# Begun feed-forward and gate blocks: another block's first half between a block's two halves, and planner durations and ranks set per sequence

## The chip, the cores and the metric

The kernel runs as one program on one core of a Trainium2 chip. The metric is the device time of one execution in microseconds (us), as the median of several runs.

The core has five engines that work side by side, each through its own queue in order: TensorE (PE, matmul), VectorE (DVE), ScalarE (ACT), GpSimd (POOL) and SyncE (SP, which here issues the DMA transfers). Semaphores tie them together. An instruction that waits holds up everything behind it on its engine.

## The reference, cut to what matters

The layer is computed for two sequences of 512 tokens of width 1024 that share all weights: a prompt (s = 0) and a sample (s = 1).

```
x = x + 0.5 * swiglu(rms_norm(x, ffn1_norm), w_gate, w_up, w_down)       # width 2816 inside
h = rms_norm(x, mix_norm);  proj = h @ w_in
aq, ak, av, mq, mk, mv, gate_pre, o_pre, g_att, g_mlstm = split(proj)
att = gqa_block_attention(rope(rms_norm(aq)), rope(rms_norm(ak)), av)    # 8 heads of 64, 2 of keys and values
mem = mlstm_bidirectional(mq, mk, mv, gate_pre, bias, o_pre, head_norm)  # 4 heads of 128, both directions
merged = sigmoid(g_att) * (att @ w_up_att) + sigmoid(g_mlstm) * (mem @ w_up_mlstm)
x = x + merged @ w_out
x = x + 0.5 * swiglu(rms_norm(x, ffn2_norm), w_gate, w_up, w_down)
y = rms_norm(x, final_norm)
```

## The kernel before

**Products.** Every fp32 operand is split in two parts (high, and what is left), and each product is three matmuls: high with high, high with low, low with high. The high part is made on ACT and the low part on DVE; for a weight of 128 x 1024 that is L817 and L820 in the mixing block, L2086 and L2089 in the blocks below, L247 and L248 in the feed-forwards. The gates and the feed-forwards multiply by a scheme of seven products instead of eight over the two sequences: the activations are held as blocks B11, B21, B22 and sums T1 to T4, the weights likewise, and results are put together afterwards.

**Three stages in time.** The first feed-forward fills the first 646 us of the trace, the second the last 603 us; their instruction order is written out by hand. Between them lies the planned stage: the gates g_att and g_mlstm of both sequences (about 646 to 772 us), the mixing block of the prompt (to 1034 us), that of the sample (to 1408 us), and the begun part of the second feed-forward (to 1453 us).

**The planner** (`Plan`, L707 to L768) sets the order in the planned stage when the program is built. Each piece of work is a task with an engine, a duration, what it depends on, and slots that it needs and frees: `mm=3`, `ps=2`, `pt=2`, `o=1` are PSUM banks, `w=2` and `wr=4` weight buffers, `kr=2` rows that hold results until a DMA has stored them. An engine takes, among the tasks that could start by its model clock first, the one of lowest rank. The rank is a base value, plus 0.001 for each task entered earlier, plus an entry of the table `RANK` (L693) under the key "part engine function". Durations come from `ACT_STEP` and `DVE_STEP` (L774, L775) by width and from a count n; a matmul of 512 columns counts 0.227; a transfer is taken to land `LANDING` = 1.9 after its bytes have moved. The planner's numbers set the order only. On the chip an engine runs in that order, whenever its semaphores allow.

**A begun block** (`begun_block`, L2108) is the part of a block of results that needs only B11 and B21, the sample's sums being unready. There are eight for the gates (`begin_gates`, L2231, part "gates7") and seven for the second feed-forward (`begin`, L2339, part "begin"). Each has two halves. The first half is 12 matmuls on B11 into a new `mm` bank (`seven`, L2093; the matmul is L2100); then ACT copies the bank to a `kr` row (`out`, L2128) and a DMA stores it. The second half is 12 matmuls on B21 that add to the same bank, so they may start only when that copy has read it; then a second ACT instruction at L2128 (Tanh for the gates, Silu for the feed-forward) frees the bank. All matmuls of `seven` have the base rank FILL = 5.

**The sums** (`sums_stage`, L2133, parts "gsums" and "sums") run on the other engines beside the begun blocks: scaling of rows (ACT L2140, DVE L2141), turns, that is transposes on PE (L1690), their copies with a gain (ACT L2170), stores of copied halves to xn1buf for later (DMA, L2178), differences (DVE L2190) that overwrite those halves, and the high and low parts of each sum (`put_in`: ACT L2182, DVE L2185).

**The rest of the gates** (`gates_rest`, L2249) multiplies the sums with sums of weights made on DVE (`left_sums`, four instructions). Its first product, p1, waits for its weights, the sums of T2, and the last begun block (`begun_g[-1]`).

**The mixing block** (`mix(s, ...)`, L878 to L1640) names the parts of its work by `do.part` ("kv", "k", "q", "gates", "keys", "rotate", "attend", "memory" and so on), one name for both sequences. Lines of it that are spoken of: queries are normalised and rotated on DVE (L1097 to L1111, low part L1131), turned on PE (L1137) and copied on ACT (L1140); scores (L1213) pass Exp on ACT (L1225), which needs a table load there. In "memory", the squares of a head are turned (`sums_`, L1523), summed (`reduced`, L1527), their root taken by 11 DVE instructions (`rooted`, L172 to L167), spread on PE (`cast`, L188) and applied (`ended`, L1536). The up-projections (L838) are merged on DVE (L1381), which frees their `mm` bank.

## Time and profile before

| | |
|---|---|
| time, median of 3 runs (lowest to highest) | 2056.19 us (2055.44 to 2056.62) |
| time of the profiled execution | 2058.12 us |
| its span | 2056.0 us |
| mean granted clock of TensorE | 0.998 |
| PE busy | 2030.5 us, 99%, 9370 matmuls |
| DVE, ACT, POOL busy | 1599.3, 966.2, 27.3 us |
| bytes moved by DMA | 389.04 MB, mean 189 GB/s |

The span runs from the first to the last instruction; the execution's own time is 2.12 us longer. Matmuls are pipelined, so a busy row of PE shows each as about 0.39 us although they start some 0.23 us apart; an idle time of PE shown in brackets is therefore less than what the matmul came late by. The better measure is from one start to the next, against the pace of matmuls that wait for nothing. In the listings in order of time a row reads: start, us, engine, line, operation, out<-in, count, and in brackets the idle time before and what ended it.

### The profile page before, as it was taken

What the parts mean: (1) busy time and instruction counts of PE and PEld (TensorE: products, weight loads), DVE (VectorE), ACT (ScalarE), POOL (GpSimd) and SP (SyncE); (2) the same over time, 40 slices, a digit from 0 to 9 for tenths busy, and PEclk for the clock granted to TensorE, in tenths of its full rate; (3) what the DMA queues carried; (4) which work ended last, traced back from release to release, by engine and by line L of the source; (5) the groups of instructions that cost most, each with busy time, mean ns of one, the idle gap of its engine ahead of it and who ended that gap; (6) DMA issues with size and microseconds to landing.
All of it is one profiled execution on the core that took longest, in us unless ns stands there. A gap on an engine that the chain in (4) does not pass through costs nothing.

```text
span 2056.0 us, 26145 instructions
## 1 busy us (share of the span) xinstructions
PE 2030.5 (99%) x9370; PEld 1679.7 (82%) x9370; DVE 1599.3 (78%) x2536; ACT 966.2 (47%) x1613; POOL 27.3 (1%) x53
## 2 busy tenths in 40 slices
PE   9999999999999999999999999999999999999997
PEld 7788888888888788887888888887788888888886
DVE  7897878786797764897887885875888787776687
ACT  7444434342227533586645674655443444443224
POOL 0000000001000000000000000000000000000001
PEclk9999999999999999999999999999999999999999
DMA  9456455699774544322332512464464644379753
GB/s 338 169 172 232 174 195 197 246 363 354 251 249 158 205 147 158 104 61 83 130 122 102 191 62 93 144 222 142 138 228 156 231 163 154 134 296 396 268 201 139
DMA packets 148978, 389.04 MB, mean 189 GB/s; under 512 B 14736, under 2 KB 14752, under 8 KB 147056
## 3 DMA queue, kind: packets, MB, share of 16 engines
q1 hardware_dynamic: 147856, 385.31, 52.9%
q0 software_dynamic: 560, 1.26, 0.3%
q8 instruction: 74, 1.21, 0.2%
q10 hardware_dynamic: 432, 0.79, 0.1%
q14 instruction: 56, 0.46, 0.1%
HBM read 269.31 MB, written 118.00 MB: 188 GB/s over the span
## 4 chain that ended last, share of the span: by engine, by line
PE 92%; ACT 3%; DVE 3%; DMA 1%; issue 1%; SPq 0%; ACTq 0%; DVEq 0%
PE pss L290 18%; PE pst L290 12%; PE mm L838 10%; PE mm L290 9%; PE mm L544 8%; PE mm L868 7%; PE pst L544 4%; PE pss L544 4%; PE pss L2100 3%; PE pso L544 3%; PE pst L2100 2%; PE pso L868 2%; PE mm L2100 2%; PE pss L1213 1%; PE pst L1237 1%; PE pss L1429 1%
## 5 line engine op out<-in xcount | busy, mean ns | idle before, releaser
L290 PE MATMUL pss<-xc,w 128*128 128x512 f32 x1632 | 389.1, 390 | 0.0
L290 PEld LDWEIGHTS pss<-xc,w 128*128 128x128 f32 x1632 | 306.5, 188 | 63.6 <-ACT w L247 0.2
L247 ACT ACTIVATE w<-wr 128x1024 fp32r<-128x1024 f32 (+1 forms) x122 | 127.3, 1045 | 227.2 <-PE pst L290 128.1
L248 DVE TENSOR_TENSOR w<-wr,w 128x1024 fp32r<-128x1024 f32 (+1 forms) x122 | 146.8, 1205 | 63.7 <-ACT w L247 63.2
L290 PE MATMUL mm<-xc,w 128*128 128x512 f32 x792 | 192.3, 393 | 2.9 <-DVE w L248 1.8
L544 PE MATMUL mm<-w,rt 128*128 128x512 f32 x792 | 185.3, 390 | 0.0
L290 PEld LDWEIGHTS mm<-xc,w 128*128 128x128 f32 x792 | 149.4, 189 | 35.5 <-DVE w L248 2.2
L544 PEld LDWEIGHTS mm<-w,rt 128*128 128x128 f32 x792 | 148.6, 188 | 30.7
L290 PE MATMUL pst<-xc,w 128*128 128x512 f32 x528 | 127.2, 390 | 0.7 <-DVE xc L1814 0.7
L290 PE MATMUL pst<-xc,f 128*128 128x512 f32 x528 | 127.1, 390 | 0.0
L820 DVE TENSOR_TENSOR w<-wr,w 128x1024 fp32r<-128x1024 f32 (+1 forms) x80 | 93.6, 1172 | 30.0 <-ACT w L817 29.7
L290 PEld LDWEIGHTS pst<-xc,w 128*128 128x128 f32 x528 | 99.1, 188 | 21.6 <-DVE xc L1814 1.2
L290 PEld LDWEIGHTS pst<-xc,f 128*128 128x128 f32 x528 | 99.4, 188 | 20.6
L604 ACT ACTIVATE w<-t 128x512 fp32r<-128x512 f32 x82 | 51.6, 632 | 121.7 <-PE pst L544 63.6
L604 ACT ACTIVATE w<-wr 128x512 fp32r<-128x512 f32 x72 | 44.6, 631 | 128.6 <-PE pso L544 67.6
L544 PE MATMUL pss<-w,rt 128*128 128x512 f32 x396 | 94.4, 390 | 0.8 <-ACT w L604 0.8
L544 PE MATMUL pst<-w,rt 128*128 128x512 f32 x396 | 94.0, 389 | 0.0
L817 ACT ACTIVATE w<-wr 128x1024 fp32r<-128x1024 f32 (+1 forms) x80 | 80.6, 1013 | 25.1 <-PE mm L838 6.7
L2100 PE MATMUL mm<-xc,w 128*128 128x512 f32 x360 | 86.0, 394 | 4.2 <-ACT f L2128 4.2
L544 PEld LDWEIGHTS pss<-w,rt 128*128 128x128 f32 x396 | 74.3, 188 | 16.5 <-ACT w L604 1.2
L544 PEld LDWEIGHTS pst<-w,rt 128*128 128x128 f32 x396 | 74.4, 188 | 15.4
L2100 PEld LDWEIGHTS mm<-xc,w 128*128 128x128 f32 x360 | 66.7, 188 | 20.7 <-ACT f L2128 7.2
(409 smaller groups left out, 3906.3 us busy)
## 6 DMA issues: line engine op xcount, KB each, us to landing
rt<-rbuf SPq DMA_DIRECT2D x154, 512.0 KB, 5.7
rbuf<-t SPq DMA_DIRECT2D x72, 512.0 KB, 3.3
wr<-in_ffn_w_gate_dram SPq DMA_DIRECT2D x60, 512.0 KB, 4.2
wr<-in_w_in_cols_dram SPq DMA_DIRECT2D x48, 512.0 KB, 4.0
wr<-in_ffn_w_up_dram SPq DMA_DIRECT2D x44, 512.0 KB, 3.5
rbuf<-f SPq DMA_DIRECT2D x30, 512.0 KB, 3.8
rbuf<-tab SPq DMA_DIRECT2D x30, 512.0 KB, 4.0
wr<-in_ffn_w_down_dram SPq DMA_DIRECT2D x48, 256.0 KB, 5.7
```

What stands on the lines that cost most here:

```text
L247: pin(nc.scalar.activation(t[:, 0], src, AF.Copy))
L248: pin(V_.tensor_tensor(t[:, 1], src, f(t[:, 0]), op=ALU.subtract))
L290: pin(nc.tensor.matmul(p, a[:, k, :], xt[:, b, k, :], start=(first and k == 0 and i == 0), stop=(k == HK_ - 1 and i == 2), skip_group_chec ...
L544: nc.tensor.matmul(p, r[:, b, d * P:(d + 1) * P], u[:, a, :], start=(first and q == 0 and k == 0), stop=(q == len(us) - 1 and k == 2), ski ...
L604: nc.scalar.activation(hi, src, AF.Copy)
L817: own(nc.scalar.activation(c["hi"], c["raw"], AF.Copy))
L820: own(V_.tensor_tensor(c["lo"], c["raw"], f(c["hi"]), op=ALU.subtract))
L838: own(nc.tensor.matmul(b["p"], w_[:, k, cols], x_, start=(k == 0 and i == 0), stop=(k == n - 1 and i == 2)))
L868: own(nc.tensor.matmul(b[q][:, :N], x_[:, q * P:(q + 1) * P], w_[:, kl, :], start=(k == 0 and i == 0), stop=(k == KD - 1 and i == 2)))
L1213: own(nc.tensor.matmul(p, G["qT"][:, h, b * P:(b + 1) * P], G["kv"][:, h // 4 * 2 + j, :], start=(j == 0), stop=(j == 1)))
L1237: own(nc.tensor.transpose(p[:, b * P:(b + 1) * P], G["e", h, b // 2][:, b % 2, kb * P:(kb + 1) * P], ident))
L2100: own(nc.tensor.matmul(bank[name], left()[a][:, k, :], xcl[m][:, y, k, :], start=bool(first) and k == 0 and i == 0, stop=(k == HK_ - 1 and ...
```

## The change

It adds no instruction and removes none: both programs have 9370 matmuls, 7 loads of ACT tables and the same DMAs. It changes the planner's input in four ways.

1. `seven` takes `later`, added to the rank of its matmuls. `begun_block` passes 0.04 for its second half (`BEHIND`), which is as much as 40 tasks entered later.
2. p1 of `gates_rest` no longer waits for the last begun block.
3. Parts of the mixing block carry the sequence's number ("kv0", "kv1"), and the table `RANK` is replaced: 39 entries for both sequences become 49, nearly all for one sequence.
4. Some durations: `ACT_STEP` for 256, 384, 512 and 544 columns, and n of six chains of small DVE instructions.

```
-    RANK = {"gates7 ACT out": -6.5, "gates7 ACT p_high": -23.5, "gsums ACT copy": 0.19, "grest ACT a_high": -1.5,
...
+    RANK = {"gsums ACT copy": 2.5, "q0 SP w_fetch": -6.4, "q0 ACT w_high": -8.5, "gates0 PE turn_e": 45,
...
-    ACT_STEP = {8: 0.2, 32: 0.2, 128: 0.3, 256: 0.37, 384: 0.5, 512: 0.5, 544: 0.57, 1024: 0.97}
+    ACT_STEP = {8: 0.2, 32: 0.2, 128: 0.3, 256: 0.33, 384: 0.45, 512: 0.51, 544: 0.7, 1024: 0.97}
...
-        do.part = "kv"
+        do.part = f"kv{s}"
...
-        t = dve(8, k_root, [t], 1, n=24)
+        t = dve(8, k_root, [t], 1, n=20)
...
-        root_q = dve(32, hold("rq", lambda: rstd_cols(G["ssq"], 32, DA, own)), reds, 0, n=12)
+        root_q = dve(32, hold("rq", lambda: rstd_cols(G["ssq"], 32, DA, own)), reds, 0, n=18)
...
-        scaled = dve(32, scales, [u], 1, (), ["pt"], n=14)
+        scaled = dve(32, scales, [u], 1, (), ["pt"], n=20)
...
-            inv = dve(8, inverse, stt + [en_t], 0, n=4)
+            inv = dve(8, inverse, stt + [en_t], 0, n=5)
...
-            u = dve(8, rooted, [u], 0, n=24)
+            u = dve(8, rooted, [u], 0, n=20)
...
-    def seven(left, xcl, m, bank, deps, first, need=(), free=(), name="p", stop=None):
+    def seven(left, xcl, m, bank, deps, first, need=(), free=(), name="p", later=0.0):
...
-                       FILL, need if k == 0 and i == 0 else (), free if end else ())
+                       FILL + later, need if k == 0 and i == 0 else (), free if end else ())
         return t
+
+    BEHIND = 0.04
...
-                      () if a else ["mm"], ["w"] if a else ())
+                      () if a else ["mm"], ["w"] if a else (), later=a * BEHIND)
...
-        u = dve(512, left_sums, [*fetched, g_t], 2, ["lone"], n=4)
+        u = dve(512, left_sums, [*fetched, g_t], 2, ["lone"], n=5)
...
-        p1 = seven(lambda: part(wb["t"], 0), xg, T2_, bank, [wb_t, *sums_g[T2_], begun_g[-1]], PS, ["ps"], (), "Y")
+        p1 = seven(lambda: part(wb["t"], 0), xg, T2_, bank, [wb_t, *sums_g[T2_]], PS, ["ps"], (), "Y")
```

The new lines shift the numbers: L2100 becomes L2104, L2128 becomes L2134, L2140 becomes L2146, L2170 becomes L2176, L2182 becomes L2188, L1690 becomes L1694, L838 becomes L842, L1523 becomes L1527.

**First place: PE, the last begun blocks of the gates.** Before, with blocks mm_389 and mm_393; xc_313 is B11 (first half), xc_314 is B21 (second half):

```order
L2100 MATMUL mm_388_5062<-xc_313_4673,w_383_4976 128x512 x6
L2100 MATMUL mm_389_5099<-xc_313_4673,w_385_5016 128x512 x5
L2100 MATMUL mm_388_5062<-xc_314_4674,w_383_4976 128x512 x12
L2100 MATMUL mm_389_5099<-xc_313_4673,w_385_5016 128x512 x7
L2100 MATMUL mm_393_5140<-xc_313_4673,w_387_5057 128x512 x5
L2100 MATMUL mm_389_5099<-xc_314_4674,w_385_5016 128x512 x12
L2100 MATMUL mm_393_5140<-xc_313_4673,w_387_5057 128x512 x7
L2100 MATMUL mm_393_5140<-xc_314_4674,w_387_5057 128x512 x12
```

After, the last rows of the same blocks, there named mm_389 and mm_390:

```order
L2104 MATMUL mm_389_5096<-xc_313_4673,w_386_5034 128x512 x9
L2104 MATMUL mm_387_5058<-xc_314_4674,w_384_4996 128x512 x9
L2104 MATMUL mm_390_5131<-xc_313_4673,w_388_5078 128x512
L2104 MATMUL mm_387_5058<-xc_314_4674,w_384_4996 128x512
...
L2104 MATMUL mm_390_5131<-xc_313_4673,w_388_5078 128x512 x9
L2104 MATMUL mm_389_5096<-xc_314_4674,w_386_5034 128x512 x12
L2104 MATMUL mm_390_5131<-xc_314_4674,w_388_5078 128x512 x12
```

Before, 0 to 7 matmuls of the next block's first half stand between the end of a block's first half and the start of its second (5 for mm_388 and mm_389, none for mm_393). After, 24 stand there (12 of the second half of the block before, taken in turn with 12 of the first half of the block behind), and 12 for the last block.

**Second place: ACT, in the begun part of the second feed-forward.** L2140 is the scaling of rows, L2170 the copies of the turns, and the table load is that of Silu. Before:

```order
L2128 ACTIVATE f2_1413_11448<-mm_1435_11641 128x512
L2140 ACTIVATE rows_1408_11430<-rows_1408_11430,rs_1443_11685 128x2x512 x2
L2128 ACT_TABLE_LOAD
L2128 ACTIVATE f2_1413_11448<-mm_1435_11641 128x512
L2128 ACTIVATE f2_1413_11448<-mm_1437_11669 128x512
L2086 ACTIVATE w_1452_11739<-wr_1432_11597 128x1024
L2170 ACTIVATE t2_1416_11451<-pss_1450_11727,gain_3_94 128x512
L2170 ACTIVATE t2_1417_11452<-pst_1451_11734,gain_3_94 128x512
```

After:

```order
L2134 ACTIVATE f2_1413_11466<-mm_1435_11641 128x512
L2134 ACTIVATE f2_1413_11466<-mm_1437_11669 128x512
L2146 ACTIVATE rows_1405_11387<-rows_1405_11387,rs_1443_11685 128x2x512 x2
L2176 ACTIVATE t2_1416_11469<-pss_1450_11728,gain_3_94 128x512
L2176 ACTIVATE t2_1417_11470<-pst_1451_11733,gain_3_94 128x512
L2176 ACTIVATE t2_1416_11469<-pss_1452_11739,gain_3_94 128x512
L2176 ACTIVATE t2_1417_11470<-pst_1453_11745,gain_3_94 128x512
L2176 ACTIVATE t2_1418_11471<-pss_1454_11750,gain_3_94 128x512
L2188 ACTIVATE xc_1445_11716<-t2_1417_11470 128x1024
L2176 ACTIVATE t2_1418_11471<-pss_1456_11763,gain_3_94 128x512
L2134 ACT_TABLE_LOAD
L2134 ACTIVATE f2_1413_11466<-mm_1435_11641 128x512
```

The table load, the Silu and a weight split (L2086) stood ahead of the first copy of a turn; now the copies stand ahead of them.

**Third place: PE, the end of the sample's mixing block.** `att` and `mem` are what the up-projections read, pst_1351 holds the turned squares of the last head, pst_1362 its cast. Before:

```order
L1523 MATMUL pst_1351_11058<-ident_85,t2_1349_11050 128x128 x4
L838 MATMUL mm_1345_11028<-att_1049_9365,w_1329_10954 128x512 x2
L838 MATMUL mm_1353_11068<-mem_1191_10000,w_1348_11043 128x512 x9
L838 MATMUL mm_1360_11097<-mem_1191_10000,w_1348_11043 128x512 x9
L838 MATMUL mm_1361_11108<-att_1049_9365,w_1329_10954 128x512
L188 MATMUL pst_1362_11110<-ident_85,rs_1359_11089 128x128 x4
L838 MATMUL mm_1361_11108<-att_1049_9365,w_1329_10954 128x512 x11
L838 MATMUL mm_1364_11133<-mem_1191_10000,w_1350_11055 128x512 x3
L838 MATMUL mm_1353_11068<-mem_1191_10000,w_1348_11043 128x512 x3
```

After:

```order
L1527 MATMUL pst_1351_11053<-ident_85,t2_1349_11044 128x128 x4
L842 MATMUL mm_1348_11041<-att_1038_9329,w_1329_10952 128x512 x7
L842 MATMUL mm_1354_11070<-att_1038_9329,w_1329_10952 128x512 x12
L842 MATMUL mm_1360_11100<-mem_1201_10059,w_1347_11038 128x512 x4
L188 MATMUL pst_1362_11108<-ident_85,rs_1359_11088 128x128 x4
L842 MATMUL mm_1360_11100<-mem_1201_10059,w_1347_11038 128x512 x5
L842 MATMUL mm_1364_11123<-mem_1201_10059,w_1347_11038 128x512 x9
L842 MATMUL mm_1365_11136<-mem_1201_10059,w_1350_11049 128x512 x5
L842 MATMUL mm_1360_11100<-mem_1201_10059,w_1347_11038 128x512 x3
```

Before, the last block on `att` (mm_1361) ended right ahead of mm_1364, which needs one of the three `mm` banks while mm_1353 and mm_1360 still hold two. After, both last blocks on `att` (mm_1348 and mm_1354) are through before the blocks on `mem` begin.

More of the change, by code (lines that the diff above doesn't have):

```diff
@@ L978, in mix @@
         swap(k_set, (), ["x"])
-        do.part = "q"
+        do.part = f"q{s}"
         qraw, reds, sqs = [], [], []
@@ L1012, in mix @@
         box_t = swap([q_t], ["A"], ["bx", "bx"], box)
-        do.part = "gates"
+        do.part = f"gates{s}"
         Fs, Is, fa, Lt, et = [small(32, t) for t in ("Fs", "Is", "fa", "Lt", "et")]
@@ L1170, in out_gate @@
         def out_gate(h):
-            do.part = "out_gate"
+            do.part = f"out_gate{s}"
             def done(bk, t):
@@ L1202, in mix @@
             out_gate(h)
-        do.part = "attend"
+        do.part = f"attend{s}"
         exps, low, last_a = {}, {}, []
@@ L1386, in mix @@
             mem_qk(h, v_in)
-        do.part = "memory"
+        do.part = f"memory{s}"
         mem_in, mt_last, mem_banks, exps_all = [], [], [], []
@@ L1548, in mix @@
         box_free = swap(mem_in + exps_all, ["bx", "bx"], ["A", "A"])
-        do.part = "before"
+        do.part = f"before{s}"
         fresh_in = before([att_free])
@@ L1560, in mem_gate @@
         def mem_gate(i):
-            do.part = "mem_gate"
+            do.part = f"mem_gate{s}"
             def g_fetch():
@@ L1590, in mix @@
         if s:
-            do.part = "last"
+            do.part = f"last{s}"
             swap(w3, ["qk", "qk"], ["w", "w"])
```

40 lines of the change are left out of this document (19 added, 21 removed), and 6 rows, old and new, of the table RANK.

## The prediction

> **What bounds the kernel.** I read the page first, then the waits of PE by line, then the stages, then PE, ACT and DVE in order of time around each wait.
>
> ```profile
> PE 2030.5 (99%) x9370; PEld 1679.7 (82%) x9370; DVE 1599.3 (78%) x2536; ACT 966.2 (47%) x1613; POOL 27.3 (1%) x53
> PE 92%; ACT 3%; DVE 3%; DMA 1%; issue 1%; SPq 0%; ACTq 0%; DVEq 0%
> ```
>
> PE is busy 99% of the span and carries 92% of the chain that ended last. The change leaves PE its 9370 matmuls, so only PE's waiting can move. Where it waits (engine, line, what for: us in total, times, longest us):
>
> ```profile
> PE mm L2100 <- ACT f L2128: 4.2, 6, 1.1
> PE pst L1137 <- ACT qT L1140: 0.9, 1, 0.9
> PE mm L838 <- DVE mg L1381: 0.9, 1, 0.9
> ```
>
> The begun blocks hold the largest sum: 4.2 us in six waits for the copy between two halves. The stages, by window (us, busy time and count of PE, PEld, DVE, ACT, POOL, granted clock, DMA share, GB/s):
>
> ```profile
> 646.00:700.00 54.00, 51.47 (x238) 41.27 (x237) 42.76 (x54) 38.44 (x54) 0.00 (x0) 1.00 0.55 189
> 772.00:1034.00 262.00, 260.54 (x1333) 216.52 (x1332) 196.68 (x420) 158.86 (x338) 1.37 (x10) 1.00 0.32 105
> 1034.00:1408.00 374.00, 372.08 (x1854) 310.06 (x1853) 280.54 (x553) 212.61 (x424) 1.37 (x10) 1.00 0.40 134
> 1408.00:1453.00 45.00, 42.32 (x198) 33.82 (x197) 34.39 (x44) 32.38 (x44) 0.00 (x0) 1.00 0.51 169
> ```
>
> PE is idle 2.53 us in the gates, 1.46 and 1.92 us in the two mixing blocks, 2.68 us in the begun feed-forward: 8.6 us together. That is nearly all that this change can touch. Each wait costs a little more than its idle time, because the pipeline must refill, so I price waits by start times. The pace of undisturbed matmuls:
>
> ```profile
> 700.94 2.88 PE L2100 MATMUL pst<-xc,f 128*128 128x512 f32 x12
> 703.66 3.79 PE L2100 MATMUL pss<-xc,w 128*128 128x512 f32 x16
> ```
>
> Twelve take 2.72 us from start to start, 0.227 us each.
>
> **Begun blocks of the gates.** PE in order of time:
>
> ```profile
> 659.07 7.30 PE L2100 MATMUL mm<-xc,w 128*128 128x512 f32 x31
> 666.76 16.20 PE L2100 MATMUL mm<-xc,w 128*128 128x512 f32 x70 [0.38 <-ACT f L2128]
> 683.55 10.04 PE L2100 MATMUL mm<-xc,w 128*128 128x512 f32 x43 [0.59 <-ACT f L2128]
> 694.69 3.02 PE L2100 MATMUL mm<-xc,w 128*128 128x512 f32 x12 [1.10 <-ACT f L2128]
> ```
>
> 31 matmuls from 659.07 would end their pace at 666.11; the next came at 666.76, 0.65 late. Likewise 70 from 666.76 give 682.65 (0.90 late) and 43 from 683.55 give 693.31 (1.38 late): 2.93 us. By the order, 7, 5 and 0 matmuls stood between the two halves there, 1.59, 1.13 and 0 us. So the copies let PE go 2.2, 2.0 and 1.4 us after the first half had had its pace. The new order puts 24 matmuls there, 5.44 us, and 12, 2.72 us, ahead of the last. All three latenesses are below that.
>
> The danger is that the copy itself comes later. ACT works in order, and a part of a sum stands ahead of it, which waits for a difference on DVE, which waits for the store of the very half that it overwrites:
>
> ```profile
> 663.73 1.06 ACT L2182 ACTIVATE xc<-t 128x1024 fp32r<-128x1024 f32 x1 [3.65 <-DVE t L2190]
> xn1buf<-t SPq DMA_DIRECT2D x4, 512.0 KB, 5.6
> ```
>
> The store lands 5.6 us after its issue, and ACT stood still for 3.65 us. With one part of 1.06 us behind it and a copy of about 0.6 us the whole hold is 5.3 us, just under the new 5.44. So I take 2.93 us as gained; the other end is a hold of two parts (6.4 us), 0.9 us at each of the two places where xn1buf is stored, a gain of 1.1. [...]
>
> Against this gain stands the first turn, which waits for the scaling of rows:
>
> ```profile
> 654.00 0.49 PE L1690 MATMUL pss<-ident,xs 128*128 128x128 f32 x3
> 654.82 0.33 PE L1690 MATMUL pss<-ident,xs 128*128 128x128 f32 x1 [0.33 <-ACT xs L2140]
> ```
>
> It came 0.5 us late (three transposes take 0.33 from start to start). The order begins the turns after 25 matmuls of the first blocks instead of 34, 2.0 us earlier, but has both scalings on ACT ahead of any weight split, which stood between them (1 us). So I put 1.1 in the new order, a loss of 0.6 (between 0 and 2.0, all of the shift). p1's dropped wait is worth nothing: the last block still stands ahead of it. **Gates: −2.3 us** (−0.1 to −2.9).
>
> **Begun blocks of the second feed-forward.**
>
> ```profile
> 1417.24 0.94 PE L2100 MATMUL mm<-xc,w 128*128 128x512 f32 x3
> 1418.72 0.65 PE L1690 MATMUL pss<-ident,rows 128*128 128x128 f32 x4 [0.54 <-ACT t L2170]
> 1420.86 12.30 PE L2100 MATMUL mm<-xc,w 128*128 128x512 f32 x53
> 1433.48 5.51 PE L2100 MATMUL mm<-xc,w 128*128 128x512 f32 x23 [0.31 <-ACT f L2128]
> 1439.84 6.41 PE L2100 MATMUL mm<-xc,w 128*128 128x512 f32 x27 [0.85 <-ACT f L2128]
> 1447.21 6.04 PE L2100 MATMUL mm<-xc,w 128*128 128x512 f32 x24 [0.96 <-ACT f L2128]
> 1414.76 1.28 ACT L2128 ACT_TABLE_LOAD   x1
> 1444.18 0.60 ACT L2128 ACTIVATE f<-mm 128x512 f32<-128x512 f32 x1 [3.45 <-DMA kept<-f]
> ```
>
> By the same sums PE came 0.59, 1.14 and 1.24 us late at 1433.48, 1439.84 and 1447.21, with 10, 9 and 12 matmuls between the halves: the copies were 2.9, 3.2 and 4.0 us late. Note the last: with a full first half between (2.72 us) it still stalled, because ACT had waited 3.45 us for a row whose store had not landed. So 12 would not do; the 24 of the new order (5.44 us) leave 1.4 us. Only the last pair has 12 between, and by a lateness like 2.9 costs 0.2. The turn at 1418.72 came 0.80 late (1417.24 and three paces are 1417.92); the table load of 1.28 us, the Silu and the split that stood ahead of its copy now stand behind, so 0.80 goes. In its new place the load costs nothing by the rows: from the first turn, six copies of some 0.57 us, one part of a sum (1.0), the load (1.28) and the Silu (0.6) end after 7.1 us with the lags between engines, and the bank that they free is asked for after eight turns and 20 matmuls, 8.0 us. **−3.5 us** (0.80 + 0.59 + 1.14 + 1.24 less 0.2; −1.5 if half of the holds lengthen).
>
> The Trainium skill, page "ScalarE: Activation LUTs", section "What ACT_TABLE_LOAD costs", puts 1.38 us of drain beside the 1.28 of the load. By that, as an estimate, the Silu ends at 8.5 us, PE stalls 0.5 there, and the stage gives 3.0 instead of 3.5. The trace shows the 1.28 of the load and no such drain, so I stay with 3.5.
>
> **Mixing blocks.**
>
> ```profile
> 847.54 0.69 DVE L998 TENSOR_REDUCE ssq<-t 128x8 f32<-128x512 f32 x1
> 856.27 0.42 DVE L1131 TENSOR_TENSOR t<-t,t 128x256 fp32r<-128x256 f32 x1
> 853.72 2.66 PE L838 MATMUL mm<-xc,w 128*128 128x512 f32 x11
> 856.83 0.63 PE L1137 MATMUL pst<-ident,t 128*128 128x128 f32 x4 [0.46 <-DVE t L1131]
> 1119.17 0.40 PE L868 MATMUL mm<-w,mh 128*128 128x512 f32 x1
> 1120.47 0.66 PE L1137 MATMUL pst<-ident,t 128*128 128x128 f32 x4 [0.91 <-ACT qT L1140]
> 1119.83 0.59 ACT L1140 ACTIVATE qT<-pst 128x512 fp32r<-128x512 f32 x1
> 1338.33 2.77 PE L838 MATMUL mm<-att,w 128*128 128x512 f32 x11
> 1341.97 2.32 PE L838 MATMUL mm<-mem,w 128*128 128x512 f32 x9 [0.87 <-DVE mg L1381]
> ```
>
> - 856.83, prompt's queries: 0.61 late. Between the end of the sums of squares and this turn the new order has 50 matmuls and 12 transposes, 12.65 us, instead of 46 matmuls, 10.4 (from 845.8 by the pace). The chain to the end of the low part at 856.69 took 10.9 from there, most of it on DVE. By the order it gains a weight split and a second low part in place of one scaling, about 1 us: 11.9, covered. −0.6 (0 if it isn't).
> - 1120.47, sample's queries: 1.07 late (1119.17 and one pace are 1119.40). The copy at 1119.83 stood behind the Exp's table load, the Exp and a weight split; in the new order it stands ahead of the load. −1.07.
> - 1341.97, last head: 1.14 late. The block on `att` that ended just before held the third bank until its merge on DVE. In the new order both such blocks are through first, and 9 matmuls and a cast (2.5 us) pass before a bank of theirs is asked for. −1.14.
>
> What the new order of some 640 us of mixing adds in waits, the trace of before cannot show. The bounds: 0, and as much idle time as these two blocks had, 1.46 + 1.92 = 3.4 us. The nearest rows are the heads of "memory":
>
> ```profile
> 1332.73 0.60 PE L1523 MATMUL pst<-ident,t 128*128 128x128 f32 x4
> 1336.55 0.17 DVE L167 SCALAR_TENSOR_TENSOR rs<-rs,rs 128x4 f32<-128x4 f32 x1
> 1336.63 2.36 DVE L820 TENSOR_TENSOR w<-wr,w 128x1024 fp32r<-128x1024 f32 x2
> 1337.98 0.60 PE L188 MATMUL pst<-ident,rs 128*128 128x128 f32 x4
> ```
>
> From the turn of the squares to the end of the root is 4.0 us here, with a merge between; PE asked 5.25 us after. The root's shorter planned duration draws the cast nearer: by the order, 4.0 to 4.7 us of matmuls stand there in five of eight heads. That leaves 0 to 0.7 us, and one DVE instruction of 0.7 us more takes it. I take 1.7 us, the middle.
>
> **The sum.** −2.3 − 3.5 − 0.6 − 1.07 − 1.14 + 1.7 = −6.9 us. The profiled execution's own time was 2058.12 us, which becomes 2051.2; the median of the runs is 1.93 us below it, 2056.19, and becomes **2049.3 us**. Both feed-forwards are untouched.
>
> **The rivals.**
>
> *The hold moves along (0.15).* ACT reaches each copy later because more parts of sums and stores bunch ahead of it: the gates give 1.1 less 0.6, the begun feed-forward 1.5; with −2.8 and +1.7 for the mixing blocks, −3.1: 2053 us. For it: the 4.0 us lateness behind a full half. Against: 24 matmuls. That the halves aren't parted at all is ruled out by the order, which has 24 between them in all but the first and last block of each stage, and 12 in those.
>
> *The mixing blocks take back what they and the stages gain (0.15).* Waits of 6 to 8 us in place of the 1.7, spread over the casts, the turned queries and the bank merges: −8.6 + 7.6 = −1, 2055 us. For it: the slack of 0 to 0.7 us at five casts, and 0.75 us at the covered turn. Against: under the old order, too, some places were tight, and all of them together made 3.4 us.
>
> *Slower through the casts (0.10).* Two weight splits on DVE between the sum of squares and the root, 2.36 us in the row above, against a slack of 0.3: 2.1 us and 0.3 for the refill in each of eight heads, 19 us, less 8.6: 2066 us. It decides from 1.6 us a head, where 13 us eat the gain and 4 us more. Against: by the order only one of eight heads has one split (1.22 us) there, and its cast has 5.6 us.
>
> *No new wait at all (0.10).* −8.6 us: 2047.5 us.
>
> **How the numbers follow.** The forecast holds 0.50. About 0.2%, some 4 us, is what a measurement can tell from no change here: faster means below 2052.1, slower above 2060.3. The forecast's own range is 2046 to 2052, all faster; with the clean case and a third of the first rival, 0.65. Same: the rest of that rival, the second, 0.25. Slower: 0.10. The range at 8 in 10 takes in the forecast, the clean case and the first rival and most of the second: 2045 to 2056.5.
>
> **What would show it.** The waits of PE on the copy of the begun blocks fall from 4.2 us to under 1; the window of the gates has PE idle under 1.5 us instead of 2.53, that of the begun feed-forward under 1 instead of 2.68. No wait on L1144 before the sample's Exp, none on L1385 at the end. New waits in the mixing blocks sum to about 1.7 us beside the old ones left. Wrong I would be if ACT still stood over 5 us ahead of a copy, or if the casts (L188) showed up among PE's waits with over 3 us.

## The result and the profile after

The changed kernel takes 2051.81 us (median of 13 runs, 2048.39 to 2055.87), beside 2056.62 us (2054.55 to 2060.54, 13 runs) for the kernel before on the same chip: ratio 0.9974, 95% interval 0.9967 to 0.9982. The forecast was 2049.3. The profiled execution took 2052.77 us, its span is 2051.0.

The page of the changed kernel, busy time and shares of the chain that ended last:

```profile
PE 2029.0 (99%) x9370; PEld 1679.5 (82%) x9370; DVE 1596.3 (78%) x2536; ACT 964.0 (47%) x1613; POOL 27.1 (1%) x53
PE 92%; DVE 4%; DMA 2%; ACT 2%; issue 1%; SPq 0%; ACTq 0%; DVEq 0%
```

TensorE still carries 92%. What it waits for in the planned stage (us in total, times, longest us):

```profile
PE mm L2104 <- ACT f L2134: 2.2, 2, 1.3
PE pss L2104 <- DVE w L2093: 0.3, 1, 0.3
PE pst L1141 <- DVE t L1135: 0.2, 1, 0.2
```

The six waits for the copy between two halves (4.2 us) have become two waits for ACT (2.2 us), one of them for such a copy and the other, as shown below, for a bank. The wait for the sample's query copy (L1144) and for the merge at the end (L1385) are gone, and a small one for weights has come. The same windows as before:

```profile
646.00:700.00 54.00, 52.64 (x249) 43.03 (x248) 39.59 (x51) 37.66 (x54) 0.00 (x0) 1.00 0.55 188
772.00:1034.00 262.00, 260.85 (x1337) 217.09 (x1336) 197.94 (x423) 159.43 (x340) 1.34 (x10) 1.00 0.32 107
1034.00:1408.00 374.00, 373.85 (x1864) 312.03 (x1863) 280.00 (x556) 211.95 (x424) 2.32 (x10) 1.00 0.39 135
1408.00:1453.00 45.00, 43.66 (x210) 36.35 (x209) 37.91 (x45) 32.27 (x43) 0.00 (x0) 1.00 0.58 192
```

TensorE's idle time fell from 2.53, 1.46, 1.92 and 2.68 us to 1.36, 1.15, 0.15 and 1.34. The sample's mixing block now hardly waits at all; both begun stages keep half of what they had.

Idle time leaves out what a wait costs at its ends, so every run below is also given by stage, from the start of a stage's first matmul to that of the next stage's. "To the end" is the span without the first feed-forward, whose code is the same in all kernels and which took anything from 643.9 to 648.3 us.

| us | first feed-forward | begun gates | rest of gates | prompt's mixing | sample's mixing | begun feed-forward | second feed-forward | to the end | time | ratio to before |
|---|---|---|---|---|---|---|---|---|---|---|
| before | 646.16 | 51.39 | 98.94 | 265.73 | 343.50 | 47.38 | 602.90 | 1409.84 | | |
| after | 647.51 | 49.55 | 99.78 | 264.69 | 341.31 | 44.69 | 603.44 | 1403.46 | 2051.81 | 0.9974 [0.9967, 0.9982] |
| after_again | 646.53 | 49.06 | 99.79 | 264.76 | 341.27 | 45.15 | 603.42 | 1403.45 | 2051.65 | 0.9974 [0.9963, 0.9984] |
| no_later | 646.85 | 52.27 | 98.64 | 264.81 | 341.68 | 46.96 | 603.01 | 1407.37 | 2055.02 | 0.9985 [0.9976, 0.9993] |
| later_only | 646.71 | 49.65 | 103.52 | 265.81 | 343.56 | 47.30 | 603.30 | 1413.14 | 2060.46 | 1.0012 [1.0003, 1.0020] |
| rank_out | 647.72 | 49.89 | 99.10 | 265.77 | 343.23 | 45.57 | 602.55 | 1406.11 | 2054.82 | 0.9990 [0.9980, 1.0000] |
| half_cover | 647.22 | 49.90 | 98.70 | 264.77 | 341.52 | 44.28 | 606.29 | 1405.46 | 2052.56 | 0.9975 [0.9966, 0.9985] |
| ranks_only | 646.51 | 52.52 | 98.73 | 270.16 | 350.56 | 39.67 | 610.60 | 1422.24 | 2071.23 | 1.0061 [1.0046, 1.0077] |
| land_late | 648.25 | 48.33 | 99.79 | 264.76 | 341.69 | 44.55 | 603.45 | 1402.57 | 2049.89 | 0.9961 [0.9949, 0.9974] |
| last_copy_first | 646.71 | 49.13 | 99.79 | 264.73 | 341.43 | 43.07 | 604.39 | 1402.54 | 2051.06 | 0.9973 [0.9963, 0.9984] |
| land_late_last | 643.88 | 48.34 | 99.79 | 264.73 | 341.22 | 43.09 | 604.79 | 1401.96 | 2048.47 | 0.9960 [0.9948, 0.9972] |
| three_edits | 645.76 | 48.34 | 99.39 | 264.69 | 341.05 | 43.06 | 604.67 | 1401.20 | 2048.52 | 0.9954 [0.9942, 0.9967] |

Times are medians, in us, each to be read beside the runs of the kernel before that shared its chip (2056.6 to 2058.1 us); the ratio does that. In half_cover and ranks_only part of the begun work is done behind the start of a later stage, so from the begun feed-forward on only "to the end" can be compared there.

From before to after the five planned stages, 806.93 us, became 800.01: 6.92 less. The span fell only 5.0, as in this one execution the first feed-forward took 1.35 and the second 0.54 more.

Where the begun stages still wait. PE, then ACT and DVE, in order of time in the begun gates:

```profile
654.27 0.33 PE L1694 MATMUL pss<-ident,xs 128*128 128x128 f32 x1 [0.44 <-ACT xs L2146]
659.46 22.26 PE L2104 MATMUL mm<-xc,w 128*128 128x512 f32 x97
682.64 14.58 PE L2104 MATMUL mm<-xc,w 128*128 128x512 f32 x63 [0.92 <-ACT f L2134]
676.35 1.10 ACT L2188 ACTIVATE xc<-t 128x1024 fp32r<-128x1024 f32 x1
681.04 1.06 ACT L2188 ACTIVATE xc<-t 128x1024 fp32r<-128x1024 f32 x1 [3.59 <-DVE t L2196]
682.01 0.58 ACT L2134 ACTIVATE f<-mm 128x512 f32<-128x512 f32 x1
683.43 0.58 ACT L2134 ACTIVATE f<-mm 128x512 f32<-128x512 f32 x1
679.78 1.23 DVE L2196 TENSOR_TENSOR t<-t,t 128x1024 f32<-128x1024 f32 x1 [2.28 <-DMA xn1buf<-t]
```

97 matmuls from 659.46 would have ended their pace at 681.45; the next came at 682.64, 1.19 late. By the order, that next matmul is not a second half: it is the first one of a new block (mm_389 on B11), which needs one of the three `mm` banks. The ACT instruction at 682.01 is the second one of an older block (mm_383), the Tanh that frees its bank. It stands third behind two parts of sums, and the second of them waited 3.59 us for a subtraction on DVE that waited for the store to xn1buf. From 676.35 to the end of the Tanh ACT was held 6.24 us. Between the last matmul of mm_383 and the first of mm_389 stand 18 matmuls, 4.08 us by the pace, and not the 24 that part two halves. The copy between two halves (mm_387) came next, at 683.43; its second half started at 686.17, without a wait.

The same in the begun feed-forward, PE and then ACT:

```profile
1412.66 0.60 PE L1694 MATMUL pss<-ident,rows 128*128 128x128 f32 x4
1416.31 27.02 PE L2104 MATMUL mm<-xc,w 128*128 128x512 f32 x118
1444.66 3.02 PE L2104 MATMUL mm<-xc,w 128*128 128x512 f32 x12 [1.33 <-ACT f L2134]
1443.07 1.06 ACT L2090 ACTIVATE w<-wr 128x1024 fp32r<-128x1024 f32 x1 [2.92 <-DVE wr L2375]
1444.03 0.58 ACT L2134 ACTIVATE f<-mm 128x512 f32<-128x512 f32 x1
```

The turns run without a wait and 118 matmuls without a break; then the last pair's second half comes 1.60 late (1416.31 and 118 paces are 1443.06). Here it is the copy between the two halves, with 12 matmuls between. It stood behind a weight split that waited 2.92 us for the left sums on DVE.

### The profile page after: what moved, and what is told of

Same layout as the page of the kernel before. It is cut to its first block, busy times and chain, and to the rows that moved or that the text cites. A ratio compares the mean times of both kernels' runs of the same rounds, so it can differ in the third digit from the quotient of the medians.

```text
span 2051.0 us, 26137 instructions
## 1 busy us (share of the span) xinstructions
PE 2029.0 (99%) x9370; PEld 1679.5 (82%) x9370; DVE 1596.3 (78%) x2536; ACT 964.0 (47%) x1613; POOL 27.1 (1%) x53
## 4 chain that ended last, share of the span: by engine, by line
PE 92%; DVE 4%; DMA 2%; ACT 2%; issue 1%; SPq 0%; ACTq 0%; DVEq 0%
PE pss L290 18%; PE pst L290 12%; PE mm L842 10%; PE mm L544 8%; PE mm L290 7%; PE mm L872 7%; PE pst L544 4%; PE pss L544 4%; PE mm L2104 3%; PE pss L2104 3%; PE pso L544 3%; PE pso L872 2%; PE pst L2104 2%; PE pss L1217 1%; PE pst L1241 1%; PE pss L1433 1%
## 5 line engine op out<-in xcount | busy, mean ns | idle before, releaser
L2104 PE MATMUL mm<-xc,w 128*128 128x512 f32 x360 | 84.2, 392 | 2.2 <-ACT f L2134 2.2
L2104 PEld LDWEIGHTS mm<-xc,w 128*128 128x128 f32 x360 | 67.1, 188 | 16.9 <-ACT f L2134 3.1
```

Source lines behind the costliest of these rows:

```text
L2104: own(nc.tensor.matmul(bank[name], left()[a][:, k, :], xcl[m][:, y, k, :], start=bool(first) and k == 0 and i == 0, stop=(k == HK_ - 1 and ...
```

## The experiments

### The changed kernel once more

after_again is the changed kernel, unchanged.

> The changed kernel once more, as the yardstick of this group. In the first pair of profiles the planned stage (first matmul of the gates to first matmul of the second feed-forward) went from 806.9 to 800.0 us, but the medians fell by 4.8 us only, because the first feed-forward, which is the same code, took 1.35 us longer in the profile of after and the second 0.5 us. Theory A (the feed-forwards vary from run to run): planned stage again 800.0 within 0.5, the feed-forwards elsewhere between 645.5 and 648 and between 602.5 and 604. Theory B (the new order makes the feed-forwards slower): again 647.5 and 603.4 or more.

Its planned stages sum to 800.03 us against 800.01. The begun stages repeat only to 0.5 us each: the stall in the gates was 0.71 us here instead of 1.19, that of the last pair 2.02 instead of 1.60. That the sum repeats to 0.02 is luck, as the two differences cancel; the other planned stages repeat to 0.07. Its first feed-forward took 646.53, so theory A holds for that part. The second took 603.42 as in the first profile of the change; in no_later, later_only and land_late, too, it took 603.0 to 603.5 against the 602.90 of before. Whether some 0.5 us is given back there stays open, since rank_out has 602.55.

### One part alone: the later second half

later_only is the kernel before with only the later rank of the second halves; the mixing blocks keep their old order.

```
-                       FILL, need if k == 0 and i == 0 else (), free if end else ())
+                       FILL + later, need if k == 0 and i == 0 else (), free if end else ())
...
+    BEHIND = 0.04
...
-                      () if a else ["mm"], ["w"] if a else ())
+                      () if a else ["mm"], ["w"] if a else (), later=a * BEHIND)
```

> Before, with the second halves ranked later and nothing else; by the order, the mixing blocks are those of before. Theory A (the distance between the halves gives the gain of the begun blocks by itself): begun gates 49.5 instead of 51.4 us, begun feed-forward 44.7 instead of 47.4, mixing blocks as before; about 4.5 us less in all. Theory B (the table and the durations are needed too, because they set when ACT reaches the copies): half of it, about 2 us less, with waits of PE on L2128 of over 2.5 us.

Both theories missed: this part alone makes the kernel slower, by 0.12% (0.03 to 0.20). The begun gates do gain 1.74 us, but the rest of the gates loses 4.58, and the begun feed-forward, 44.7 by theory A, keeps its length with 47.30. PE and DVE in order of time there:

```profile
696.36 0.61 PE L2100 MATMUL pss<-xc,w 128*128 128x512 f32 x2
699.88 4.33 PE L2100 MATMUL pss<-xc,w 128*128 128x512 f32 x12 [2.91 <-DVE w L2089]
695.82 0.69 DVE L2264 TENSOR_TENSOR t<-wr 128x512 f32<-128x512 f32 x1
698.00 0.69 DVE L2267 TENSOR_TENSOR wr<-wr 128x512 f32<-128x512 f32 x1
698.61 4.62 DVE L2089 TENSOR_TENSOR w<-wr,w 128x1024 fp32r<-128x1024 f32 x4
```

PE stood 3.07 us for the low part of the first weight pair. On DVE the second chain of left sums (695.82 to 698.69) went ahead of it. And the 12 matmuls behind the stall took 4.33 us instead of some 2.9; the windows (granted clock is the third number from the end) show why:

```profile
700.00:702.00 2.00, 2.00 (x8) 1.58 (x9) 2.00 (x2) 0.73 (x1) 0.00 (x0) 0.82 0.51 174
702.00:704.00 2.00, 2.00 (x6) 1.53 (x5) 1.83 (x3) 0.00 (x0) 0.00 (x0) 0.50 0.86 274
```

The clock fell to half behind the standstill. The price of the stall was 3.07 us and 1.6 more.

### One number more: the rank that sets DVE's order

rank_out is later_only without one old entry of the table, an entry that the change drops as well.

```
-    RANK = {"gates7 ACT out": -6.5, "gates7 ACT p_high": -23.5, "gsums ACT copy": 0.19, "grest ACT a_high": -1.5,
+    RANK = {"gates7 ACT out": -6.5, "gates7 ACT p_high": -23.5, "gsums ACT copy": 0.19,
```

> The run later_only with a single number less: the rank of -1.5 for the later gate weights' high splits (grest ACT a_high) is left out of the table of before; the changed durations and ranks stay out too, and the mixing blocks keep the order of before. In the order of work the split of the first weight pair that the remaining gates need then stands on VectorE ahead of the second chain of left sums, as in the changed kernel. Theory A (the 3.07 us standstill of later_only and the 1.6 us of half clock behind it come from that one place in VectorE's row): remaining gates 99.8 +-0.6 us instead of 103.52, no granted clock under 0.9 there, begun gates about 49.6, begun feed-forward still about 47.3, the run some 3.7 us under later_only: 2056.7, no different from before. Theory B (the second half put later holds back the copies that free banks and buffers, whatever VectorE's order, so that the wait comes back elsewhere): remaining gates at or over 102.5, the run at 2059 to 2061.

DVE and PE at the same place:

```profile
696.72 1.22 DVE L2089 TENSOR_TENSOR w<-wr,w 128x1024 fp32r<-128x1024 f32 x1 [2.51 <-ACT w L2086]
698.58 0.69 DVE L2264 TENSOR_TENSOR t<-wr 128x512 f32<-128x512 f32 x1
697.61 2.95 PE L2100 MATMUL pss<-xc,w 128*128 128x512 f32 x12
```

The split now goes ahead of the second left sums and PE doesn't wait. The rest of the gates takes 99.10 us, a little under theory A's band, instead of 103.52, and the kernel goes from 1.0012 to 0.9990. So the cost of the later halves in the rest of the gates hung on that entry. To the end the kernel is 3.73 us shorter than before, but in time it can't be told from it (0.9980 to 1.0000). Theory A expected 47.3 in the begun feed-forward; it came to 45.57. There both kernels stall at the last pair for nearly as long (2.28 and 2.40 us late), but the granted clock stayed at 1.00 here, and fell to 0.55 and 0.60 in two windows of 2 us behind the stall in later_only. Here:

```profile
1448.43 3.01 PE L2100 MATMUL mm<-xc,w 128*128 128x512 f32 x12 [2.12 <-ACT f L2130]
```

and in later_only:

```profile
1452.11 4.60 PE L2100 MATMUL mm<-xc,w 128*128 128x512 f32 x12 [2.23 <-ACT f L2130]
```

### The other part alone, and a smaller added rank

no_later and half_cover are the changed kernel with another `BEHIND`:

```
-    BEHIND = 0.04
+    BEHIND = 0.0
```

and 0.016. By the order, the eight blocks of the gates then have 5, 5, 7, 7, 6, 5, 5 and 0 matmuls between their halves in no_later, and 5, 5, 10, 6, 5, 8, 5 and 0 in half_cover: nearly the same. The last four blocks of the feed-forward have 11, 10, 12 and 12, and 10, 5, 9 and 2.

> After, with BEHIND = 0 (the table, the durations and p1 as after); by the order, the mixing blocks are those of after and the begun blocks nearly those of before. Theory A: begun gates 51.4 and begun feed-forward 47.4 us as before, PE waiting about 4 us on L2134, mixing blocks 1.0 and 2.2 us shorter than before; about 3 us less in all than before. Theory B (the table and the durations do most of it): over 4.5 us less than before.

> After, with BEHIND = 0.016; by the order, 5 to 10 matmuls of the next block stand between the two halves instead of 24 (in the begun feed-forward mostly 9 or 10). Theory A (copies come 2 to 4 us after the first half, so it takes about 20 matmuls to hide them): waits of PE on L2134 of 2.5 to 4.5 us, as before, and no gain in the begun feed-forward against before (47.4 us). Theory B (any first half between is enough): waits under 2.2 us and a time like that of after.

The waits for the copy, first in no_later:

```profile
PE mm L2104 <- ACT f L2134: 5.2, 5, 1.4
```

and in half_cover:

```profile
PE mm L2104 <- ACT f L2134: 2.2, 4, 0.8
```

PE of half_cover in order of time:

```profile
658.60 34.90 PE L2104 MATMUL mm<-xc,w 128*128 128x512 f32 x151
694.27 3.02 PE L2104 MATMUL mm<-xc,w 128*128 128x512 f32 x12 [0.77 <-ACT f L2134]
1430.31 4.60 PE L2104 MATMUL mm<-xc,w 128*128 128x512 f32 x19 [0.73 <-ACT f L2134]
1435.35 10.06 PE L2104 MATMUL mm<-xc,w 128*128 128x512 f32 x43 [0.44 <-ACT f L2134]
```

Without the distance the waits are back: five, 5.2 us, beside six and 4.2 us before. The mixing blocks keep their gain, so the two parts are apart, as theory A had it: the tables (ranks and durations) alone are worth 2.5 us to the end, and the distance 3.9 more.

In half_cover the begun gates run 151 matmuls with one start only 0.24 late among them, and the last block, with no matmul between its halves, stalls. That stage takes 49.90 us, near the 49.06 and 49.55 of the change, where no_later takes 52.27. So 24 matmuls were more than needed there. The step from no_later is small: that run stalls at three blocks, the last with no matmul between; at the other two three matmuls more stand between in half_cover, and at the first of them the copy, too, came sooner, as the second half could start 2.5 us after the first half instead of 3.1. Why wasn't followed up. In the feed-forward a second half stalls behind 10 matmuls (0.89 late) and behind 5 (0.60), while 9 were enough twice. The waits, 2.2 us, lie at the edge of theory B, and in time half_cover can't be told from the change (0.9975 beside 0.9974), though in its one profile it is 2.0 us longer to the end. So neither theory holds in both stages, and how much of the gain needs 24 is open.

### The ranks without the durations

ranks_only is no_later with all durations of before:

```
-    ACT_STEP = {8: 0.2, 32: 0.2, 128: 0.3, 256: 0.33, 384: 0.45, 512: 0.51, 544: 0.7, 1024: 0.97}
+    ACT_STEP = {8: 0.2, 32: 0.2, 128: 0.3, 256: 0.37, 384: 0.5, 512: 0.5, 544: 0.57, 1024: 0.97}
...
-        t = dve(8, k_root, [t], 1, n=20)
+        t = dve(8, k_root, [t], 1, n=24)
```

(and the five other counts likewise).

> The changed kernel without the later rank of the second half (BEHIND = 0) and with all durations of before: the new table of ranks per sequence is what is left of the change, apart from p1's dropped wait, which moves no instruction. To be compared with no_later, which has the new ranks and the new durations and has mixing blocks of 264.8 and 341.7 us, 606.5 together, where before has 609.2. Theory A (the gain of the mixing blocks comes from the new ranks, and the durations only shift the model clock a little): mixing blocks 606.0 to 607.0 us. Theory B (the ranks are worth something only with the durations beside them): in the order of work two of the sample's query copies stand ahead of the Exp's table load and two turns behind it, as before, so the wait of 1.07 us at L1144 comes back, and other places are as unprepared; mixing blocks 607.8 to 610 us. The begun blocks under both as in no_later, 52.3 and 47.0 within 0.7.

Theory B, and by more than it said: 14.9 us more to the end than no_later. Its two windows of mixing, and then some of its waits:

```profile
772.00:1034.00 262.00, 257.78 (x1307) 212.24 (x1306) 194.24 (x415) 156.25 (x335) 1.35 (x10) 1.00 0.33 106
1034.00:1408.00 374.00, 367.76 (x1829) 303.77 (x1828) 277.79 (x555) 210.63 (x419) 2.40 (x10) 1.00 0.39 130
```

```profile
PE mm L872 <- DVE w L824: 2.4, 2, 1.8
PE pss L1217 <- ACT t L1229: 1.9, 3, 1.4
PE pso L1507 <- ACT t L1496: 1.1, 1, 1.1
```

4.2 and 6.2 us of idle time, in many small waits for weights, scores and exponentials. The turned queries (L1141, L1144), which theory B had named, are not the large ones. What the new durations do with the old ranks wasn't run. (The old table has 38 entries and the new one 53, by the code.)

### What holds ACT at the last two stalls

land_late tells the planner that the store to xn1buf takes 2.5 us longer; nothing on the chip waits for more.

```
+                    out[i] = [do("POOL", 0.0, 2.5, lambda: None, out[i], 0)]
```

> The changed kernel with one task in the planner that lasts 2.5 us behind the store of the summed input of the begun blocks, so that the split of the landed input is put later in ScalarE's and VectorE's rows; nothing on the chip waits for more. In the changed kernel a bank's copy stands behind that split, which waits 3.59 us for VectorE, which waits 2.28 us for the landing, and TensorE stands 1.19 us in the begun gates. Theory A (the planner holds the landing for shorter than it is, 1.9 us against 4.4 to 7.2 in the traces, and the order that follows blocks the copy): the stall of 1.19 goes, begun gates 49.1 to 49.6 becomes 48.0 to 48.5, the remaining gates within 0.5 of 99.8; whole 2050.5. Theory B (the later split is what the remaining gates need, and the wait moves there): begun gates fall by 1.1, remaining gates grow by 0.8 or more, whole within 0.5 of the changed kernel's 2051.7.

last_copy_first ranks the splits of the next weights lower:

```
-    RANK = {"gsums ACT copy": 2.5, "q0 SP w_fetch": -6.4,
+    RANK = {"gsums ACT copy": 2.5, "next ACT p_high": 2, "q0 SP w_fetch": -6.4,
```

> The changed kernel with one rank more (next ACT p_high: 2), which puts ScalarE's copies of the last begun feed-forward block ahead of the splits of the next feed-forward's weights; in the changed kernel the copy that frees the last block's bank stands behind a split that waits 2.92 us for VectorE's left sums, and TensorE stands 1.61 us at the last pair. Theory A (the copy is late only because of its place in ScalarE's row): the stall at the last pair goes, begun feed-forward 44.69 to 45.15 becomes 43.2 to 43.8, the wait of the first product of the feed-forward for its weights grows by at most 0.7 since VectorE's split of the weights now stands behind one more subtraction; the whole 1 to 1.5 us under the changed kernel, 2050.4 beside its 2051.7. Theory B (the left sums bound the end of this stage, not the copy): the first product of the feed-forward waits for VectorE's split as long as the last pair waited before, 1.2 to 1.6 us, and the stage with the first two blocks of the feed-forward keeps its length within 0.3.

land_late_last has both.

> Both edits, the landing held for longer by 2.5 us and the copies of the last block ahead of the weights' splits. Theory A of both: the two gains add, planned stages 797.0 to 798.3 us instead of 800.0, whole 2048.7 to 2050.0 beside the changed kernel's 2051.7. Theory B of both: within 0.5 of the changed kernel.

PE in the begun gates of land_late:

```profile
660.20 36.54 PE L2104 MATMUL mm<-xc,w 128*128 128x512 f32 x160
696.58 2.97 PE L2104 MATMUL pss<-xc,w 128*128 128x512 f32 x12
```

160 matmuls in one piece, up to the first product of the rest: the stall of 1.19 is gone, as the Tanh that frees the bank now runs ahead of the split (at 678.77), the begun gates take 48.33, and the rest takes 99.79 as in the change. Theory A. PE and ACT in the begun feed-forward of last_copy_first:

```profile
1419.70 25.32 PE L2104 MATMUL mm<-xc,w 128*128 128x512 f32 x111
1445.86 2.56 PE L290 MATMUL pss<-xc,w 128*128 128x512 f32 x10 [0.39 <-DVE w L2093]
1440.05 0.60 ACT L2134 ACTIVATE f<-mm 128x512 f32<-128x512 f32 x1 [0.72 <-DMA kept<-f]
1441.83 2.01 ACT L2090 ACTIVATE w<-wr 128x1024 fp32r<-128x1024 f32 x2 [1.19 <-DVE wr L2375]
```

The copy is done before the split and the stage takes 43.07 us, 1.6 to 2.1 less. But 0.95 of it comes back in the second feed-forward (604.39): its first product starts 0.55 late for the split that stands one subtraction later, and another matmul, at 1456.91, is 0.49 late for DVE (L327). Theory A for the stall, theory B for about half of its worth; in time (0.9973) the edit can't be told from the change. Both edits together: 797.17 us for the planned stages, in theory A's band, but 1.35 come back in the second feed-forward, so 1401.96 to the end, 1.5 less than the change.

### The rest of the gates

three_edits adds to land_late_last a shorter count for the left sums, which lets a weight split go ahead of an addition in DVE's row.

```
-        u = dve(512, left_sums, [*fetched, g_t], 2, ["lone"], n=5)
+        u = dve(512, left_sums, [*fetched, g_t], 2, ["lone"], n=3)
```

> land_late_last with a third edit: the left sums of the remaining gates count n=3 instead of 5 in the planner, which in VectorE's row puts the low part of the second weight pair ahead of an addition on the first results (L2296), the order that rank_out has there, whose remaining gates take 99.10 us where those of land_late_last take 99.79. Theory A (TensorE's 0.5 us at the second product of the remaining gates is that addition's place): remaining gates 99.0 to 99.3 us, all other stages as in land_late_last within 0.2, planned stages 796.5 us, whole about 0.7 under land_late_last. Theory B (the weights' left sums themselves are late, and the addition hides behind them): remaining gates 99.6 to 100, no gain.

The rest of the gates takes 99.39, in between: 0.4 of the 0.84 us that the change lost there hung on that place. Of the other half, 0.33 is now at the first product, which waits at 694.88 for the low part of the first weight pair (DVE L2093). To the end it is the best kernel, 2.25 us under the change and 8.64 under before. In time (2048.52 against 2048.47) it can't be told from land_late_last.

## Why the prediction was right, and where it was not

The sum was −6.9 us for the planned stages; they became 6.92 us shorter in one profile of the change and 6.91 in the other. That agreement is luck, and better than the working behind it: two errors of 2.1 us cancelled, the mixing blocks' against that of the three other stages.

| stage | forecast | after | after_again |
|---|---|---|---|
| begun gates | −2.3 | −1.84 | −2.33 |
| rest of gates | 0 | +0.84 | +0.85 |
| begun feed-forward | −3.5 | −2.69 | −2.23 |
| both mixing blocks | −2.81 + 1.7 | −3.23 | −3.20 |
| sum | −6.9 | −6.92 | −6.91 |

**Begun gates: the size nearly right, one wait of another kind.** All three stalls of before, each at a second half, went, as the distance was to make them. In place of the middle one, 0.90 before, came one of 1.19 (0.71 in after_again). ACT was held there as I had put it at the lower end, by two parts of sums (6.24 us measured, 6.4 worked out). But I had set that hold against the 24 matmuls between two halves, and there 24 were enough. PE stood for a bank: a block whose halves lie further apart keeps its bank longer, and 18 matmuls had to cover the Tanh that frees it. For the gates my text has no term for that. Holding the store for longer in the planner removes the stall (land_late), which shows what held the Tanh. The first turn came 0.63 us late instead of the 1.1 forecast, 0.14 more than before and not 0.6, and a later turn, 0.38 late before, came nearly in time. So a gain smaller than forecast met a loss smaller than forecast. The store to xn1buf landed after 4.4, 5.6 and 7.2 us before, where three of its four landings are traced; the planner counts some 3.5 for it (0.35 for the issue, 1.28 for the bytes, and LANDING; the 1.9 set beside these times in the expectation of land_late is LANDING alone).

**How many matmuls are needed.** That 12 would not do I had said of the feed-forward, where 10 were too few in half_cover and the last pair stalled behind 12. For the gates my own figures, copies 2.2, 2.0 and 1.4 us after the first half, asked for 10 as long as the copies came no later, and in half_cover 5 to 10 were nearly enough.

**Begun feed-forward: the term of the last pair was mis-sized.** The text charged it 0.2, by a lateness of 2.9 us against the 2.72 of 12 matmuls. It cost 1.60, and 2.02 in after_again. The row that would have told was in the text: the last copy that stalled before was 4.0 us late behind a full half, which gives 1.3. I took the smaller lateness for the place that had shown the larger. The rest of the term held: turns without a wait, all other halves in one piece, the table load at no cost in its new place. The stage gained some 0.5 us beyond these terms, which I have not placed. ACT of the changed kernel around the load:

```profile
1417.12 0.71 ACT L2176 ACTIVATE t<-pss,gain 128x512 f32<-128x512 f32 x1
1417.84 1.28 ACT L2134 ACT_TABLE_LOAD   x1
1419.14 0.60 ACT L2134 ACTIVATE f<-mm 128x512 f32<-128x512 f32 x1
```

The load starts as the copy ends, and the Silu as the load ends. The Silu ends 7.08 us after the first turn (1412.66), where I had worked out 7.1. So the trace agrees with the row. It shows no sign of the 1.38 us of drain that the Trainium skill, page "ScalarE: Activation LUTs", section "What ACT_TABLE_LOAD costs", adds, and the measurement decides.

**Rest of the gates: a stage that I had put at nothing.** I spoke only of p1's dropped wait, which indeed moves nothing: with it put back, the program has the same instructions in the same order on every engine. That the second halves, put later, bring the left sums and splits close to p1's start was not in the sum; without them the stage takes 98.64 (no_later). later_only shows what could have hung on it, 4.58 us. Leaving out one old rank cures that (rank_out), and the change leaves it out as well.

**Mixing blocks: the new waits were mis-sized.** The named gains came: 1.08 and 1.03 us left the sample's block at the query copy and at the last merge (−1.07 and −1.14 forecast), while 0.40 of the prompt's 0.61 stayed. PE of the changed kernel at the prompt's turned queries:

```profile
855.64 1.52 PE L842 MATMUL mm<-xc,w 128*128 128x512 f32 x6
857.40 1.06 PE L1141 MATMUL pst<-ident,t 128*128 128x128 f32 x8 [0.24 <-DVE t L1135]
```

Six paces from 855.64 are 857.00, so the chain on DVE was not wholly covered. Of the 1.7 us of new waits only 0.69 are found as late starts (0.31 in the sample's block, 0.23 and 0.15 in the prompt's), and two old ones that I had not counted, 0.36 and 0.30, went. Together that makes some 2.3 of the 3.2 us gained; the rest I have not placed. 1.7 was only the middle between two far ends. No cast waits, as forecast.

**The signs.** PE's idle time in the window of the gates is 1.36, under the 1.5 that I had named, and no wait is left at L1144 or L1385. But the waits for ACT in the begun blocks came to 2.2 us and not under 1, PE's idle time in the begun feed-forward to 1.34 and not under 1, and the new waits in the mixing blocks to 0.69 and not 1.7.

**The rivals.** ACT was held at two places, worth 2.8 us, not everywhere. That new ranks can take back more than everything is no idle fear: without the durations that belong to them the kernel is 14.9 us longer to the end than with them and 12.4 longer than before (ranks_only), through weights, scores and exponentials rather than the casts that I had suspected.

**From the sum to the time.** 2051.8 is 2.5 over the forecast. Of that, 0.4 is the kernel before, 2056.62 in 13 runs and not the 2056.19 of three. The ratio means 5.3 us gained (3.7 to 6.8), a little less than 6.9. I had taken both feed-forwards as fixed. The second was 0.5 us longer in both profiles of the change, so that 6.4 are left to the end, within that interval. The first varies by 4.4 us over twelve profiles of the same code, so single profiles can't close the rest. Why it varies wasn't tried.

## What to carry to other kernels

Distance between two halves on TensorE helps only as far as the engine between them isn't held: look for what stands ahead of the copy in its in-order row and what that waits for, above all a store that must land, and correct the planner's figure for it. It also keeps a bank longer, so look, too, for the instruction that frees the bank. A wait on one line of code can be either: tell them apart by the block that the waiting matmul belongs to. A change of order in one stage must be followed to the first consumers of the next stage, where the same engines meet. And a term that two far ends bound is no forecast: when the sum fits, check it stage by stage before you believe the working.

## What the hardware showed beside

A stall can cost more than its length. In the twelve profiles TensorE stood for 2.1 to 3.3 us, from one start to the next (0.23 us more than a lateness as given above), 16 times. Behind ten of them seven or eight of the next matmuls took 0.2 us more, 1.4 to 1.6 us in all; behind six, one as long as 2.51 us, at most one did. Behind shorter stalls, 1.3 to 1.9 us, it didn't happen after the first 15 us of the trace. The kernel before, in the first feed-forward:

```profile
82.00:84.00 2.00, 1.51 (x5) 1.27 (x6) 1.47 (x3) 1.65 (x3) 0.00 (x0) 0.85 0.02 6
84.00:86.00 2.00, 2.00 (x6) 1.55 (x5) 2.00 (x2) 0.00 (x0) 0.00 (x0) 0.50 0.00 0
86.00:88.00 2.00, 2.00 (x8) 1.60 (x8) 2.00 (x2) 0.60 (x1) 0.00 (x0) 0.80 0.00 0
```

The Trainium skill, page "TensorE: Matmul & The Clock Gate", section "What's actually happening", has the clock halve after an idle window of about 3.4 us that runs freely. The length of the half clock here, seven or eight matmuls of 0.43 us, and that it comes behind some stalls and not others would fit such a window. But here a standstill of 2.2 us was enough, and the measurement decides. What decides between two stalls of like length these runs don't show.
